# A two-layer decoder trunk on one Trainium2 core: twelve pairs of feed-forward units a layer by seven products, with their weight sums built in scratch memory by accumulating GpSimd transfers

## The chip, the cores and the metric

One core of one Trainium2 chip runs the kernel. The metric is device time in microseconds (us). The kernel before has a median of 1816.6 us in three runs (1816.02, 1816.82, 1816.6). Engines are called as the profile calls them: PE is TensorE (PEld its weight loads), DVE is VectorE, ACT is ScalarE, POOL is GpSimd, and SP is the queue that issues most transfers.

## The reference

Two layers, each on 512 tokens of width 1024 in float32:

```python
h = rmsnorm(x, pre_mix_g)
proj = h @ w_in                                  # q,k,v,z | b,a | q,k,v | gates A, B
y_a = deltanet_branch(...) @ w_up_dn             # 8 heads, gated delta rule in chunks
y_b = swa_sink_branch(...) @ w_up_sw             # 16 heads, window 128
mix = (sigmoid(gate_a) * y_a + sigmoid(gate_b) * y_b) @ w_o
x = x + rmsnorm(mix, post_mix_g)
h2 = rmsnorm(x, pre_mlp_g)
ff = square(relu(h2 @ w_ff1)) @ w_ff2            # 1024 -> 4096 -> 1024
x = x + rmsnorm(ff, post_mlp_g)
```

## The kernel before

All matmuls work on pairs of numbers: a value x is split into a high part (rounded to the format of the fast matmul) and a low part x - high, and a product is the sum of high by high, low by high and high by low. So a plain matrix product is three matmuls per block of 128 rows of the weight (`mm_a`, lines 400 to 402: 512 columns each). Weights come from DRAM in blocks of 128 x 1024 floats (512 KB), one transfer on SP each (`load`, line 282), into one of six buffers `wr`; ACT makes the high part `wh` (line 384) and DVE the low part `wl` (line 385). `weights()` does that four blocks ahead of use (`LOOK`).

A layer runs so: the attention and beta columns of `w_in`; 16 steps of `MIX`, in which the key columns (K), the gate columns (G) and (GA) of `w_in` are multiplied while groups of attention heads run between them (POOL masks the probabilities there, line 1017, tile `pc`); `w_up_sw` (`ps_us`); then the eight delta heads; `w_up_dn` (`ps_ud`); `w_o` with its normalisation; and the feed-forward part.

**The delta heads.** For each head h a chain of four chunks runs through PE, DVE and PE again: `ps_y` (line 1264) to `yy` (DVE, line 1266) to `ps_su` (line 1269) to the state `St` (DVE, line 1272) to `ps_ks` (line 1258) to `rr` (DVE, line 1261) to the next `ps_y`. Between these small matmuls stand matmuls of the next heads' projections (`ps_vp`, `ps_qp`, `ps_zp`) or, in the last head, of the gate (`ps_ga`), so that PE has work while DVE answers. A head's result is normalised by a factor that travels through memory (`d_tail`): `ps_w` sums the squares, `sd<-w` and `ff<-sd` (SP) turn the row into 128 x 4, POOL raises it to a power (line 1215) and stores it (`fd<-ff`, line 1216, the only transfer that POOL issues), `fb<-fd` (SP, line 1219) spreads it over 128 partitions, and DVE multiplies (`yf<-yf,fb`, line 1220). The next head but one does the last step. ACT and DVE then split the result into `yT_h` and `yT_l` (lines 500 and 501) for `w_up_dn`, whose first four units take heads 0 to 5 first (4 x 6 x 3 = 72 matmuls), and then heads 6 and 7.

**The feed-forward part.** `w_ff1` has 32 units of 128 columns, in four slices s = 0 to 3 of eight. Slices 0 to 2 are multiplied by their part of `w_ff2` by seven products instead of eight (`lefts`, `mm_c`). Units of `w_ff1` are multiplied plainly, or two at a time by seven products (`ff1`, `mm_h`): with x0, x1 the two halves of the first unit and x2, x3 those of the second, the seven products need, beside x0, x1 and x3, the sums x0+x2, x0+x2+x3, x0+x1+x2+x3 and x2+x3. `up_specs` loads both units and lets DVE build the sums in two more `wr` buffers (line 343, four additions of 128 x 512 a pair). `SEQ` says which units are pairs: none in slice 0, two in slice 1, three in slice 2 and four in slice 3, nine a layer.

**What sets the order.** The kernel is traced in program order, and a scheduler then places each engine's instructions by its own estimate of when they are ready; a few chains are fixed by hand (`Order`). Transfers on SP wait for the data they need and also for the eighth transfer before them (the waits on DMAHW0 to 7 in the listings below). An engine takes its instructions strictly in order, so one that waits holds all behind it.

## Time and profile before

| what | value |
|---|---|
| runs before (median of 3) | 1816.6 us (1816.02 to 1816.82) |
| the profiled execution | 1816.19 us, its span 1814.5 us |
| PE, PEld busy | 1794.6 us (99%), 1524.7 us (84%) |
| DVE, ACT, POOL busy | 1375.1 us (76%), 1007.5 us (56%), 210.6 us (12%) |
| transfers | 278.60 MB, mean 154 GB/s |
| weight blocks of 512 KB | 320, median 3.6 us from issue to landing |

The span is the time from the first to the last instruction of the profiled execution; its own time holds 1.7 us more. Shares of busy time are averages; what a stretch is bound by is read from that stretch. A row of the timeline gives the start in us, the duration in us (matmuls overlap, so the pace is read from the starts), engine, line, operation, output <- inputs, shape, and in brackets the idle time before it and what ended that.

### The profile page before, as it was taken

What the parts mean: (1) busy time and instruction counts of PE and PEld (TensorE: products, weight loads), DVE (VectorE), ACT (ScalarE), POOL (GpSimd) and SP (SyncE); (2) the same over time, 40 slices, a digit from 0 to 9 for tenths busy, and PEclk for the clock granted to TensorE, in tenths of its full rate; (3) what the DMA queues carried; (4) which work ended last, traced back from release to release, by engine and by line L of the source; (5) the groups of instructions that cost most, each with busy time, mean ns of one, the idle gap of its engine ahead of it and who ended that gap; (6) DMA issues with size and microseconds to landing.
All of it is one profiled execution on the core that took longest, in us unless ns stands there. A gap on an engine that the chain in (4) does not pass through costs nothing.

```text
span 1814.5 us, 28394 instructions
## 1 busy us (share of the span) xinstructions
PE 1794.6 (99%) x10252; PEld 1524.7 (84%) x10252; DVE 1375.1 (76%) x2590; ACT 1007.5 (56%) x2065; POOL 210.6 (12%) x386
## 2 busy tenths in 40 slices
PE   9999999999999999999999999999999999999998
PEld 8878878888788888989898887888877888889896
DVE  5499796887666878898556997968875669698973
ACT  6678742444434656566556877234443347566572
POOL 0322102221101000000013221022111010000000
PEclk9999999999999999999999999999999999999999
DMA  5633447655463254554445334585545533555551
GB/s 201 203 112 121 111 146 226 178 172 152 117 208 129 82 164 156 174 180 145 168 160 176 106 127 111 169 232 159 163 140 154 171 116 105 174 162 164 174 178 56
DMA packets 146431, 278.60 MB, mean 154 GB/s; under 512 B 33569, under 2 KB 66657, under 8 KB 146290
## 3 DMA queue, kind: packets, MB, share of 16 engines
q1 hardware_dynamic: 145778, 276.75, 49.2%
q8 instruction: 81, 1.33, 0.3%
q14 instruction: 60, 0.49, 0.1%
q0 software_dynamic: 512, 0.03, 0.0%
HBM read 239.38 MB, written 37.36 MB: 153 GB/s over the span
## 4 chain that ended last, share of the span: by engine, by line
PE 88%; DVE 4%; ACT 4%; DMA 2%; issue 1%; POOL 0%; SPq 0%; DVEq 0%; POOLq 0%; ACTq 0%
PE ps_b L459 3%; PE ps_b L461 3%; PE ps_b L463 3%; PE ps_f L400 2%; PE ps_f L401 2%; PE ps_f L402 2%; PE ps_us L400 2%; PE ps_ud L400 2%; PE ps_us L401 2%; PE ps_ud L401 2%; PE ps_ud L402 2%; PE ps_us L402 2%; PE ps_vp L400 2%; PE ps_vp L402 2%; PE ps_vp L401 1%; PE ps_qp L401 1%
## 5 line engine op out<-in xcount | busy, mean ns | idle before, releaser
L384 ACT CAST wh<-wr 128x1024 fp32r<-128x1024 f32 (+2 forms) x368 | 372.7, 1019 | 430.4 <-PE ps_us L401 60.2
L385 DVE TENSOR_TENSOR wl<-wr,wh 128x1024 fp32r<-128x1024 f32 (+2 forms) x368 | 434.9, 1189 | 183.8 <-ACT wh L384 180.2
L526 POOL TENSOR_TENSOR pr<-pq,pw 128x1 f32<-128x1 f32 x16 | 9.8, 615 | 790.1 <-DVE pq L525 790.1
L459 PE MATMUL ps_b<-wh,h_h 128*128 128x432 f32 (+1 forms) x192 | 71.1, 370 | 0.0
L461 PE MATMUL ps_b<-wl,h_h 128*128 128x432 f32 (+1 forms) x192 | 70.4, 367 | 0.0
L463 PE MATMUL ps_b<-wh,h_l 128*128 128x432 f32 (+1 forms) x192 | 70.3, 366 | 0.0
L400 PE MATMUL ps_f<-g_h,wh 128*128 128x512 f32 x160 | 62.4, 390 | 0.0
L401 PE MATMUL ps_f<-g_l,wh 128*128 128x512 f32 x160 | 62.4, 390 | 0.0
L402 PE MATMUL ps_f<-g_h,wl 128*128 128x512 f32 x160 | 62.2, 389 | 0.0
L401 PE MATMUL ps_qp<-h_l,wh 128*128 128x512 f32 x128 | 53.9, 421 | 0.0
L400 PE MATMUL ps_vp<-h_h,wh 128*128 128x512 f32 x128 | 53.7, 420 | 0.0
L402 PE MATMUL ps_vp<-h_h,wl 128*128 128x512 f32 x128 | 53.7, 419 | 0.0
L995 ACT ACTIVATE M<-M,nm 128x128 f32<-128x128 f32 x128 | 49.8, 391 | 5.9 <-DVE nm L990 5.8
L400 PE MATMUL ps_qp<-h_h,wh 128*128 128x512 f32 x128 | 51.8, 405 | 0.0
L343 DVE TENSOR_TENSOR wr<-wr 128x512 f32<-128x512 f32 x72 | 47.5, 685 | 5.5 <-DMA wr<-in_weights_dram 5.2
L400 PE MATMUL ps_kp<-h_h,wh 128*128 128x512 f32 x128 | 51.6, 403 | 0.0
L402 PE MATMUL ps_qp<-h_h,wl 128*128 128x512 f32 x128 | 51.4, 401 | 0.0
L401 PE MATMUL ps_vp<-h_l,wh 128*128 128x512 f32 x128 | 51.3, 401 | 0.0
L401 PE MATMUL ps_ga<-h_l,wh 128*128 128x512 f32 x128 | 51.0, 398 | 0.0
L400 PE MATMUL ps_gb<-h_h,wh 128*128 128x512 f32 x128 | 51.0, 398 | 0.0
L402 PE MATMUL ps_kp<-h_h,wl 128*128 128x512 f32 x128 | 50.9, 398 | 0.0
L402 PE MATMUL ps_ga<-h_h,wl 128*128 128x512 f32 x128 | 50.7, 396 | 0.0
(435 smaller groups left out, 5928.4 us busy)
## 6 DMA issues: line engine op xcount, KB each, us to landing
wr<-in_weights_dram SPq DMA_DIRECT2D x320, 512.0 KB, 3.6
wr<-in_weights_dram SPq DMA_DIRECT2D x24, 432.0 KB, 5.2
D<-dd SPq DMA_DIRECT2D x32, 256.0 KB, 2.7
xd<-xo SPq DMA_DIRECT2D x12, 512.0 KB, 3.0
xt<-xd SPq DMA_DIRECT2D x24, 256.0 KB, 4.5
D<-gd SPq DMA_DIRECT2D x16, 256.0 KB, 6.2
dd<-D SPq DMA_DIRECT2D x16, 256.0 KB, 5.2
kkd<-kk SPq DMA_DIRECT2D x16, 256.0 KB, 2.0
```

Source lines behind the costliest of these rows:

```text
L343: tt(out=o_, in0=i0, in1=i1, op=ALU.add)
L384: nc.scalar.copy(wh[:, :w], wr[:, :w])
L385: sub(out=wl[:, :w], in0=wr[:, :w], in1=wh[:, :w].bitcast(F32), op=ALU.subtract)
L400: mm(ps, lhsT=wh[:, k, :], rhs=hi, start=k == 0, stop=False)
L401: mm(ps, lhsT=wh[:, k, :], rhs=lo, start=False, stop=False)
L402: mm(ps, lhsT=wl[:, k, :], rhs=hi, start=False, stop=k == KT - 1)
L459: mm(pss[t], lhsT=hi[:, tsl], rhs=wh[:, r, :], start=k == 0 and not onto, stop=False, skip_group_check=onto)
L461: mm(pss[t], lhsT=hi[:, tsl], rhs=wl[:, r, :], start=False, stop=False, skip_group_check=onto)
L463: mm(pss[t], lhsT=lo[:, tsl], rhs=wh[:, r, :], start=False, stop=k == KT - 1, skip_group_check=onto)
L526: ptt(out=r, in0=q1, in1=mhalf[:, 0:1], op=ALU.pow)
L995: act(out=M[:, j * P:(j + 1) * P], in_=M[:, j * P:(j + 1) * P], func=AF.Exp, bias=nm[:, j:j + 1], accum_out=den[:, j:j + 1])
```

## The change

`SEQ` makes pairs of all units in slices 1 and 2 too: twelve pairs a layer, six more in all. The sums aren't built by DVE any more. For each pair a tile `sums[l, s, pair]` of 128 x 2048 floats lies in DRAM. It is made in four steps (`prepare`): SP copies both units into it (two transfers of 512 KB from DRAM to DRAM); POOL adds to its second and fourth quarter, by one accumulating transfer, the first halves of the units (512 KB); POOL adds one quarter of the tile to another (256 KB); and once more. What stands in it then are the four sums. `unit(ms[0])` and the two halves of the tile are loaded as blocks of 512 KB, and the second half of the second unit as one of 256 KB.

`ready = prepare(l)` does one step for each of up to four pairs at a time, so that one `next(ready)` issues up to two copies on SP and three transfers on POOL. The fifteen calls stand in `MIX` (steps 1, 4, 7, 10), in two places of `w_up_sw`, at the start of heads 1, 3, 5 and 7, in two places of `w_up_dn` and in three of slice 0. `tc.keep_in_program_order` ties each of these transfers behind the instruction of its engine that was traced just before it; those traced after it are not tied. Besides, two halves of a block change places (`n1` and `n2`), the first left factor `P1` is made as soon as its units are there, and two pairs of PSUM banks change their pools in slices 1 and 2.

```diff
--- before.py
+++ after.py
@@ -42,7 +42,8 @@
 WR = 6
 FF_ORDER = (0, 4, 1, 5, 2, 6, 3, 7)
 XB = 6
-SEQ = (FF_ORDER, (0, 1, (4, 5), (2, 3), 6, 7), ((0, 1), (4, 5), (2, 3), 6, 7), ((0, 1), (2, 3), (4, 5), (6, 7)))
+FF_PAIRS = ((0, 1), (4, 5), (2, 3), (6, 7))
+SEQ = (FF_ORDER, FF_PAIRS, FF_PAIRS, ((0, 1), (2, 3), (4, 5), (6, 7)))
 
 MIX = "G K K G K K G K K G K K G GA GA GA".split()
 NA = sum(c.count("A") for c in MIX)
@@ -328,22 +329,19 @@
         def one(ms):
-            b = {}
-
-            def raw():
-                b["0"], b["1"] = (unit(m) for m in ms)
-                return b["0"]
-
-            def of(n_):
-                b[n_] = wp.tile([P, 1024], F32, name="wr", bufs=WR)
-                x0, x1, x2, x3 = b["0"][:, :512], b["0"][:, 512:], b["1"][:, :512], b["1"][:, 512:]
-                yb = b["a"][:, 512:]
-                for o_, i0, i1 in (((b[n_][:, :512], x0, x2), (yb, b[n_][:, :512], x3)) if n_ == "a" else
-                                   ((b[n_][:, 512:], x2, x3), (b[n_][:, :512], yb, x1))):
-                    tt(out=o_, in0=i0, in1=i1, op=ALU.add)
-                return b[n_]
-
-            return raw, lambda: of("a"), lambda: of("b"), lambda: b["1"][:, 512:]
+            d = sums[l, s, ms]
+
+            def of(c, w=1024):
+                wr = wp.tile([P, 1024], F32, name="wr", bufs=WR)
+                dma(wr[:, :w], d[:, c * 1024:c * 1024 + w])
+                return wr
+
+            def tail():
+                wr = wp.tile([P, 1024], F32, name="wr", bufs=WR)
+                dma(wr[:, :512], wpk[index["w_ff1", l, 0, (s * 8 + ms[1]) * P, 0], :, 512:])
+                return wr
+
+            return lambda: unit(ms[0]), lambda: of(0), lambda: of(1), tail
 
         last = None
         for n, e in enumerate(SEQ[s]):
@@ -358,6 +356,35 @@
                 out += [(fa, 0), (fb, 0)]
                 last = tail
         return out + [(last, -1)] * bool(last)
+
+    pairs = [(s_, e) for s_, seq in enumerate(SEQ) for e in seq if isinstance(e, tuple)]
+    sums = {(l, *p): dr.tile([P, 2048], F32, name=f"fs{l}{p[0]}{p[1][0]}")
+            for l in range(depth) for p in pairs}
+
+    def prepare(l):
+
+
+        here = tc.keep_in_program_order
+
+        def stages(s_, e):
+            i = index["w_ff1", l, 0, (s_ * 8 + e[0]) * P, 0]
+            assert index["w_ff1", l, 0, (s_ * 8 + e[1]) * P, 0] == i + 1
+            v = sums[l, s_, e][:, :].rearrange("p (h t c) -> p h t c", h=2, t=2)
+            for t in range(2):
+                here(dma(v[:, :, t, :], wpk[i + t].rearrange("p (h c) -> p h c", h=2)))
+            yield
+            here(pdma(v[:, :, 1, :], wpk[i:i + 2, :, 0:512].rearrange("t p c -> p t c"),
+                      accum_op=ALU.add))
+            yield
+            here(pdma(v[:, 0, 0, :], v[:, 1, 1, :], accum_op=ALU.add))
+            yield
+            here(pdma(v[:, 1, 0, :], v[:, 0, 0, :], accum_op=ALU.add))
+
+        todo = [stages(*p) for p in pairs]
+        for n in range(len(todo) + 3):
+            for g in todo[max(n - 3, 0):n + 1]:
+                next(g, None)
+            yield
 
     specs = []
     for kind_, *key in chunk_order(depth):
@@ -1041,7 +1068,10 @@
 
 
         late, klate = (), []
+        ready = prepare(l)
         for i in range(16):
+            if i in (1, 4, 7, 10):
+                next(ready)
             us = []
             for c in MIX[i]:
                 u = kind[c](n_[c])
@@ -1299,6 +1329,8 @@
             stt(out=mb, in0=sgb[m], scalar=1.0, in1=ps, op0=ALU.add, op1=ALU.mult)
             dma(mbd[m], mb)
             steps(2 if m < 6 else 40)
+            if m in (1, 4):
+                next(ready)
             if m == 1:
                 turn0()
         for m in range(NA, NA2):
@@ -1314,6 +1346,8 @@
             d_decay(h)
             d_turn(h)
         for h in range(H):
+            if h % 2:
+                next(ready)
             if h < H - 2:
                 d_keys(h + 2)
             d_inverse(h)
@@ -1340,6 +1374,8 @@
             first.append((ps, mm_a(ps, yT, range(6))))
         mT = []
         for m in range(KT):
+            if m in (1, 5):
+                next(ready)
             if m % 4 == 0:
                 mq = UQ("mbr")
                 sq = UQ("sgr") if m < NA2 else None
@@ -1504,13 +1540,13 @@
                     return c
 
                 c2 = weights()
-                mm_h(y, c2, 4, ops["n2"], False)
+                mm_h(y, c2, 0, ops["n2"], False)
                 nc.scalar.copy(z, y)
                 mm_h(a, c1, 4, ops["a12"], False)
                 act(out=R[:, half(0)], in_=a, func=AF.Relu)
                 if n > 0:
                     c3 = seventh()
-                mm_h(z, c2, 0, ops["n1"], False)
+                mm_h(z, c2, 4, ops["n1"], False)
                 if n == 0:
                     c3 = seventh()
                 act(out=R[:, half(3)], in_=z, func=AF.Copy, scale=-1.0)
@@ -1542,7 +1578,6 @@
             def lefts(X, Y):
 
                 a11, a21, a12, a22 = X[:, 0:512], X[:, 512:1024], Y[:, 0:512], Y[:, 512:1024]
-                make("P1", T[5], a11)
                 s1, s2 = T[4]("S1"), T[4]("S2")
                 tt(out=s1, in0=a21, in1=a22, op=ALU.subtract)
                 make("P5", T[7], s1)
@@ -1571,6 +1606,8 @@
                     act(out=r_, in_=ps.rearrange("p (a n) -> p a n", a=2), func=AF.Relu)
                     act(out=r_, in_=r_, func=AF.Square)
                 count[0] += len(ms)
+                if ms[-1] in (1, 3):
+                    make("P1", T[5], raw[0][:, 0:512])
                 if count[0] % 4 == 0:
                     lefts(*raw)
 
@@ -1583,12 +1620,13 @@
                         mm_a(ps, h2)
                     done((m,), ps)
                     if s == 0 and i in (1, 3, 5):
+                        next(ready, None)
                         next(cg)
             else:
                 ff1(done, pending)
-            pa = [PZ("ps_pa") for t in range(2)]
+            pa = [(PM if s else PZ)("ps_pa") for t in range(2)]
             mm_c(pa, left["P1"])
-            py = [PM("ps_py") for t in range(2)]
+            py = [(PZ if s else PM)("ps_py") for t in range(2)]
             for t in range(2):
                 act(out=py[t], in_=pa[t], func=AF.Copy, scale=-1.0)
             make_later("P2", T[5])
```

**How the order moves in the delta heads.** PE in head 3, from the first `ps_su` to the second `ps_y`; before:

```order
1725 L1269 MATMUL ps_su<-yy,kd 128x128
1726 L1276 MATMUL ps_o<-aT,yy 128x128
1727 L402 MATMUL ps_vp<-h_h,wl 128x512
1728 L400 MATMUL ps_vp<-h_h,wh 128x512
1729 L401 MATMUL ps_vp<-h_l,wh 128x512
1730 L402 MATMUL ps_vp<-h_h,wl 128x512
1731 L1258 MATMUL ps_ks<-St,kk 128x128
1732 L1259 MATMUL ps_o<-qe,St 128x128
1733 L400 MATMUL ps_vp<-h_h,wh 128x512
1734 L401 MATMUL ps_vp<-h_l,wh 128x512
1735 L1264 MATMUL ps_y<-rr,Pt 128x128
```

and after (lines are 30 higher there, those of `mm_a` 27):

```order
1733 L1299 MATMUL ps_su<-yy,kd 128x128
1734 L1306 MATMUL ps_o<-aT,yy 128x128
1735 L428 MATMUL ps_vp<-h_l,wh 128x512
1736 L429 MATMUL ps_vp<-h_h,wl 128x512
1737 L1288 MATMUL ps_ks<-St,kk 128x128
1738 L1289 MATMUL ps_o<-qe,St 128x128
1739 L427 MATMUL ps_qp<-h_h,wh 128x512
1740 L428 MATMUL ps_qp<-h_l,wh 128x512
1741 L1294 MATMUL ps_y<-rr,Pt 128x128
```

The first `ps_y` of that head is row 1719 before and row 1727 after: eight more matmuls of the projection stand ahead of it. Between `ps_o` and `ps_ks` two matmuls stand where four stood. Counted from head 2's `ps_w` to this `ps_y`, the number of projection matmuls goes from 41 to 42.

DVE in the same head, from the first `yy` to the second; before:

```order
645 L1266 COPY yy<-ps_y 128x128 [waits PE_49]
646 L385 TENSOR_TENSOR wl<-wr,wh 128x1024 [waits Activation_49]
647 L1272 COPY St<-ps_su 128x128 [waits PE_49]
648 L1220 TENSOR_TENSOR yf<-yf,fb 128x512 [waits DMAHW5_49]
649 L1261 SCALAR_TENSOR_TENSOR rr<-ps_ks,neg,vs 128x128 [waits PE_49,Activation_49]
650 L1266 COPY yy<-ps_y 128x128 [waits PE_49]
```

and after:

```order
644 L1296 COPY yy<-ps_y 128x128 [waits PE_49]
645 L1250 TENSOR_TENSOR yf<-yf,fb 128x512 [waits DMAHW2_49]
646 L1302 COPY St<-ps_su 128x128 [waits PE_49]
647 L1291 SCALAR_TENSOR_TENSOR rr<-ps_ks,neg,vs 128x128 [waits PE_49,Activation_49]
648 L412 TENSOR_TENSOR wl<-wr,wh 128x1024 [waits Activation_49]
649 L1296 COPY yy<-ps_y 128x128 [waits PE_49]
```

`yf<-yf,fb`, which waits for a transfer, stood behind `St` and now stands ahead of it; the split `wl` went behind `rr`. It is so in heads 2, 3 and 4 of both layers; in heads 5 and 6 `yf` stays behind `St`, and in head 7 it was ahead of it before as well.

**How the order moves at the end of the heads.** SP from head 7's `sd<-w` to the loads for `w_up_dn`; before:

```order
268 L1211 DMA sd<-w 1x512 [waits Activation_49]
269 L282 DMA wr<-in_weights_dram 128x1024 [waits DMAHW5_49,DVE_49]
270 L1348 DMA mbr<-mbd 128x512 [waits DMAHW6_49,PE_49]
271 L1214 DMA ff<-sd 128x4 [waits DMAHW7_49,DMAHW4_49,Pool_49]
272 L1219 DMA fb<-fd 128x512 [waits DMAHW0_49,DMASW6_49]
273 L1351 DMA sgr<-gad 128x512 [waits DMAHW1_49,PE_49]
274 L1348 DMA mbr<-mbd 128x512
275 L1351 DMA sgr<-gad 128x512 [waits DMAHW3_49]
```

and after (`fs` is a tile of sums; these two copies were traced in `w_up_dn`):

```order
299 L1241 DMA sd<-w 1x512 [waits DMAHW4_49,Activation_49]
300 L1387 DMA sgr<-gad 128x512 [waits DMAHW5_49,PE_49]
301 L1249 DMA fb<-fd 128x512 [waits DMAHW6_49,DMASW6_49]
302 L374 DMA fs_122<-in_weights_dram 256x512 [waits DMAHW7_49]
303 L1244 DMA ff<-sd 128x4 [waits DMAHW4_49,Pool_49]
304 L374 DMA fs_122<-in_weights_dram 256x512 [waits DMAHW1_49]
305 L1384 DMA mbr<-mbd 128x512 [waits DMAHW2_49]
306 L1387 DMA sgr<-gad 128x512 [waits DMAHW3_49]
```

Head 7's `ff<-sd` stood ahead of head 6's `fb<-fd`; now it stands behind that and behind a copy, and another copy follows. In heads 3 and 5 two copies stand near the reload of the keys and values (`kvx<-vxd`) and ahead of `fb<-fd`: in head 3 one on each side of the reload, in head 5 both behind it.

PE there, around head 6's `ps_w`; before:

```order
2186 L1264 MATMUL ps_y<-rr,Pt 128x128
2187 L1208 MATMUL ps_w<-w_h,ones_r 128x512
2188 L1209 MATMUL ps_w<-w_l,ones_r 128x512
2189 L400 MATMUL ps_ga<-h_h,wh 128x512
2190 L1276 MATMUL ps_o<-aT,yy 128x128
2191 L401 MATMUL ps_ga<-h_l,wh 128x512
```

and after:

```order
2193 L1294 MATMUL ps_y<-rr,Pt 128x128
2194 L1238 MATMUL ps_w<-w_h,ones_r 128x512
2195 L1239 MATMUL ps_w<-w_l,ones_r 128x512
2196 L428 MATMUL ps_ga<-h_l,wh 128x512
2197 L1306 MATMUL ps_o<-aT,yy 128x128
2198 L429 MATMUL ps_ga<-h_h,wl 128x512
```

The first `ps_ud` is row 2228 in both, so head 6's `ps_w` is followed by 36 gate matmuls before and by 29 after. Of the 15 that now stand behind the first of head 7's two `ps_w`, ten stand behind the second; it was 22 and 20.

## Prediction

> **What bounds the kernel now.** I read the page's totals and chain first, then stretches of time, then TensorE's waits, and last the timelines of the places that the change touches. The totals:
>
> ```profile
> span 1814.5 us, 28394 instructions
> ...
> PE 1794.6 (99%) x10252; PEld 1524.7 (84%) x10252; DVE 1375.1 (76%) x2590; ACT 1007.5 (56%) x2065; POOL 210.6 (12%) x386
> ...
> q1 hardware_dynamic: 145778, 276.75, 49.2%
> ...
> PE 88%; DVE 4%; ACT 4%; DMA 2%; issue 1%; POOL 0%; SPq 0%; DVEq 0%; POOLq 0%; ACTq 0%
> ```
>
> TensorE is busy for 99% of the span and is 88% of the chain. So time is won by giving it fewer columns, and lost by making it wait. By stretches (columns: engine busy, then granted clock, DMA share, GB/s), first the delta heads and then the feed-forward part of layer 0:
>
> ```profile
> 306.00:490.00 184.00, 183.09 (x1262) 148.90 (x1258) 148.26 (x302) 83.17 (x160) 32.27 (x54) 1.00 0.53 148
> ...
> 657.00:843.00 186.00, 186.00 (x1094) 165.79 (x1093) 158.76 (x198) 113.15 (x171) 0.00 (x0) 1.00 0.48 154
> ```
>
> In the feed-forward part TensorE never stops: 186.00 of 186.00. In the heads it does, a little. Three rows of its waits name who can stop it near the change:
>
> ```profile
> PE ps_y L1264 <- DVE rr L1261: 1.2, 2, 0.7
> PE ps_y L1264 <- ACT vs L1247: 0.9, 1, 0.9
> ...
> PE ps_o L1023 <- POOL pc L1017: 0.6, 1, 0.6
> ```
>
> **The change, part by part. Six more pairs.** Nine pairs a layer become twelve: two more in slice 1 and one more in slice 2, six over both layers. Plain matmuls of 512 columns and those of 256 in a pair follow each other like this on PE:
>
> ```profile
> 659.62 0.39 PE L477 MATMUL ps_pw<-wl,P_h 128*128 128x512 f32 x1
> ...
> 664.15 0.39 PE L400 MATMUL ps_f<-g_h,wh 128*128 128x512 f32 x1
> ...
> 741.73 0.28 PE L487 MATMUL ps_a<-g_h,wh 128*128 128x256 f32 x1
> ...
> 742.33 0.28 PE L490 MATMUL ps_a<-g_h,wl 128*128 128x256 f32 x1
> ```
>
> Twenty steps from 659.62 to 664.15 are 0.2267 us each, five from 741.73 to 742.33 are 0.120 us. Two plain units are 2 x 8 row blocks x 3 products = 48 matmuls, 10.88 us. A pair is 7 products x 4 x 3 = 84, 10.08 us. That is 0.80 us a pair, **-4.8 us** for six, all on the path.
>
> **The sums leave VectorE.**
>
> ```profile
> L343 DVE TENSOR_TENSOR wr<-wr 128x512 f32<-128x512 f32 x72 | 47.5, 685 | 5.5 <-DMA wr<-in_weights_dram 5.2
> ```
>
> All 72 go, 47.5 us, but in stretches where TensorE never waits: nothing. In their place a pair loads 1.83 MB (three tiles of 0.52 and one of 0.26) where it loaded 1.05; twelve pairs in some 180 us add 9.4 MB, 52 GB/s to the 154 above. I take nothing for that, nor for the earlier P1, the swapped halves and the swapped PSUM pools: the 186.00 of 186.00 says that no wait is there to be moved. If that cover goes, a late tile costs its wait once per pair.
>
> **POOL in the groups of attention.** The accumulating transfers stand among the selects that TensorE waits for. The tightest place has three of them after the second of these rows; the third row is the one transfer that POOL issues in before:
>
> ```profile
> 168.56 0.64 POOL L1017 TENSOR_SCALAR_AFFINE_SELECT pc<-pf_l 128x512 fp32r<-128x512 f32 x1 [0.16 <-DVE pf_l L501]
> 172.25 0.64 POOL L1017 TENSOR_SCALAR_AFFINE_SELECT pc<-pf_h 128x512 fp32r<-128x512 f32 x1 [3.05 <-ACT pf_h L500]
> ...
> 486.09 0.62 POOL L1216 DMA_DIRECT2D fd<-ff  x1 [0.29 <-POOL ff L1215]
> ```
>
> Three issues by 0.62 us are 1.9 in a gap of 3.05: nothing. This transfer is 2 KB and the new ones 256 to 512 KB, so the upper end is the price at which the gap overflows, below among the rivals.
>
> **The order in the delta heads.** This is where I expect the change to be paid. The front part shows it: in heads 2, 3 and 4 the factor `yf<-yf,fb` moves ahead of `St` on DVE (in head 7 it stood there already), and TensorE runs two matmuls instead of four between the `ps_o` after `ps_su` and `ps_ks`. Head 3 of layer 0 before, on PE, DVE and SP:
>
> ```profile
> 377.13 0.38 PE L1264 MATMUL ps_y<-vs,Pt 128*128 128x128 f32 x2
> ...
> 379.87 0.39 PE L1258 MATMUL ps_ks<-St,kk 128*128 128x128 f32 x2
> ```
>
> ```profile
> 377.86 0.28 DVE L1266 COPY yy<-ps_y 128x128 f32<-128x128 f32 x1
> ...
> 379.19 0.28 DVE L1272 COPY St<-ps_su 128x128 f32<-128x128 f32 x1
> 379.39 0.68 DVE L1220 TENSOR_TENSOR yf<-yf,fb 128x512 f32<-128x512 f32 x1
> ```
>
> ```profile
> 370.74 0.32 SPq L1153 DMA_DIRECT2D kvx<-vxd  x1
> ...
> 374.47 0.47 SPq L1219 DMA_DIRECT2D fb<-fd  x1
> ```
>
> `ps_ks` follows `ps_y` by 2.74 us; with two matmuls fewer it is due at 2.74 - 0.45 = 2.29. The broadcast `fb` is issued 2.66 before `ps_y`, one matmul more in after, so 2.89. How long does it take to land?
>
> ```profile
>   DMA fb<-fd: 23.4, 10
> ...
> DMA to landing us min/median/max: 4.7/4.8/4.9
> ```
>
> The second row says 4.8, from few recorded landings; the first, DVE's idle time before the factors, that they are waited for already. Counting from `ps_y`, `fb` is there at 4.8 - 2.9 = 1.9, `yf` ends at 2.6 and `St` at 2.87: TensorE waits 0.6 us and a hand-over, 0.65. The ends come from two other heads, in which DVE waited for `fb`:
>
> ```profile
> 444.56 0.32 SPq L1219 DMA_DIRECT2D fb<-fd  x1
> ...
> 1295.27 0.44 SPq L1219 DMA_DIRECT2D fb<-fd  x1
> ```
>
> ```profile
> 448.28 0.69 DVE L1220 TENSOR_TENSOR yf<-yf,fb 128x512 f32<-128x512 f32 x1 [0.49 <-DMA fb<-fd]
> ...
> 1301.31 0.69 DVE L1220 TENSOR_TENSOR yf<-yf,fb 128x512 f32<-128x512 f32 x1 [1.02 <-DMA fb<-fd]
> ```
>
> At 3.7 us (444.56 to 448.28) `fb` is early and nothing waits; at 6.0 (1295.27 to 1301.31) the wait is 1.8, of which that head already paid 0.7 at `ps_y`, the longest in the first row of waits. So five heads by 0.65 and one by 1.1: **+4.4 us**, between 0 and 6 x 1.8 - 0.7 = 10. In head 7 eight more matmuls (1.8 us) come before the first `ps_y`, which waited 0.9 for `vs`: **-0.9 us**, or 0 if copies delay its load.
>
> **Copies on SP.** In heads 3 and 5 two copies of 512 KB come between the reload of `kvx` and `fb`. 276.75 MB took 49.2% of 16 engines' 1814.5 us, 51.6 engine-us a MB, so a copy of 0.52 MB is 1.7 us on all sixteen, counted once. Before, SP issues the reload at 370.74 and `fb` at 374.47; two copies (3.4 us of traffic) put in behind the reload have 2.9 us before `fb`, which leaves 0.5. That is for head 5 in both layers, **+1.0 us**; in head 3 one of the two goes ahead of the reload and I take nothing. Ends: 0, and a whole copy in all four, 6.8.
>
> [...]
>
> **The tail of head 7.** Its normalisation has to be back before `w_up_dn` needs head 7:
>
> ```profile
> 480.31 0.48 PE L1208 MATMUL ps_w<-w_h,ones_r 128*128 128x512 f32 x1
> ...
> 489.85 0.39 PE L400 MATMUL ps_ud<-yT_h,wh 128*128 128x512 f32 x1
> ...
> 1389.17 0.39 PE L400 MATMUL ps_ud<-yT_h,wh 128*128 128x512 f32 x1
> ```
>
> ```profile
> 488.07 0.35 SPq L1214 DMA_DIRECT2D ff<-sd  x1
> 489.36 0.32 SPq L1219 DMA_DIRECT2D fb<-fd  x1
> ```
>
> ```profile
> 503.64 1.29 DVE L501 TENSOR_TENSOR yT_l<-yf,yT_h 128x512 fp32r<-128x512 f32 x2 [0.20 <-DVE yf L1220]
> ...
> 1403.47 1.29 DVE L501 TENSOR_TENSOR yT_l<-yf,yT_h 128x512 fp32r<-128x512 f32 x2 [0.20 <-DVE yf L1220]
> ```
>
> The low part is ready at 504.93; its first user is the 77th matmul, 489.85 + 76 x 0.227 = 507.1: 2.2 us of slack, and 1.7 in layer 1 (1404.76 against 1406.4). After, head 6's `ps_w` stands 7 matmuls nearer to the end (29 instead of 36), so its `fb` leaves SP at 489.36 + 1.6 = 490.96. Head 7's `ff<-sd` now stands behind that `fb` and a copy: two issues of 0.4, so 491.8 instead of 488.07, 3.7 late. TensorE waits 1.5 and 2.0: **+3.5 us**. It is 0 if what follows is quicker by 2, and 2 x 1.7 more if the copies are in the way of `ff` and `fb`.
>
> **Sum.** -4.8 + 4.4 - 0.9 + 1.0 + 3.5 = +3.2 us. On the profiled execution's 1816.19 that is 1819.4; the median of the runs, 1816.6, lies 0.4 above it: **1819.8 us**. What a measurement of this kernel can tell from no change is about 0.2%, 3.6 us, so the bounds are 1813.0 and 1820.2.
>
> **The rivals.** *The gain with few waits.* The broadcasts land like the one of 3.7 us and head 7's chain catches up: -4.8 - 0.9 and 0 to 1 of waits, **1811 us**. For it: TensorE waits little in the heads before, and most new distances are no shorter. Against: the recorded landings of 4.7 to 4.9, and the 23.4 us that DVE already idles before those factors.
>
> *Copies in the way, slower.* Each copy costs the small transfer behind it a full 1.7 us: four broadcasts (+6.8 instead of 1.0) and head 7's `ff` or `fb` in each layer (+3.4): 1819.8 + 9.2 = **1829 us**. It decides from about 0.25 us per copy on (3.2 - 1.0 + 6 x 0.25 = 3.7 is past the bound). For it speaks the 6.0 row; against it the 2.9 us of head start and DMA engines that are half idle.
>
> *POOL late.* If issuing a transfer holds POOL 1.2 us longer, three take 5.5 in the gap of 3.05, and TensorE waits 2.4 for the select, once a layer: 1819.8 + 4.8 = **1824.6 us**. [...]
>
> *No gain.* The pairs don't save their 0.8 us, because a tile of sums comes late in slice 1: 1819.8 + 4.8, also 1824.6, or about the time before where the heads cost nothing. The pairs of slice 3 speak against it.
>
> **How the numbers follow.** The forecast has 0.40, its own range being 1814 to 1824: of it 0.22 within 0.2%, 0.15 slower, 0.03 faster. Few waits: 0.32, 0.30 of it faster and 0.02 same. Copies: 0.18, slower. POOL: 0.06, 0.04 slower and 0.02 same. No gain: 0.04, half same, half slower. Together faster 0.33, same 0.28, slower 0.39. Below 1810.5 lies about a third of the second case, above 1829 half of the third: the range is 1810.5 to 1829.
>
> **What would show it.** Right: the stretch of the feed-forward part is 2.4 us shorter in each layer with TensorE still full; in heads 2, 3 and 4 `ps_ks` waits for `St`, and DVE before it for `fb`; the first `ps_ud` that uses head 7 waits for `yT_l`. Wrong: no such waits (then the time is near 1811), or waits for `pc` in the groups, or for `wr` in slice 1.

## The result and the profile after

The changed kernel takes 1876.1 us (median of four runs, 1871.8 to 1878.3) against 1816.7 for the kernel before beside it (1816.0 to 1818.3): 1.0323 times as long, 95% interval 1.0300 to 1.0345. That is slower by 59 us. The prediction named this sign as its likeliest single one (0.39), but with 1819.8 us and a range that ended at 1829. The profiled execution of after is the fastest of its four, 1871.77 us.

The totals of the page of after, and three of its DMA issues (the last columns: KB each, us to landing):

```profile
span 1870.0 us, 29142 instructions
...
PE 1805.4 (97%) x10468; PEld 1541.3 (82%) x10468; DVE 1348.1 (72%) x2542; ACT 1024.3 (55%) x2101; POOL 291.0 (16%) x458
...
PE 74%; DMA 8%; DVE 8%; ACT 4%; issue 3%; POOL 2%; SPq 0%; DVEq 0%; POOLq 0%; ACTq 0%
...
fs<-in_weights_dram SPq DMA_DIRECT2D x48, 512.0 KB, 6.3
...
fs<-in_weights_dram POOLq DMA_DIRECT2D x24, 512.0 KB, 10.7
fs<-fs POOLq DMA_DIRECT2D x48, 256.0 KB, 7.1
```

PE is busy for 97% of the span instead of 99%, and it fell from 88% to 74% of the chain; DMA went from 2% to 8%, DVE from 4% to 8%, POOL from 0% to 2%. An accumulating transfer takes 7 to 11 us from issue to landing. By stretches of layer 0: heads, `w_up_dn`, feed-forward part; first before, then after (columns as in the prediction: us, engines busy, granted clock, DMA share, GB/s):

```profile
301.26:489.85 188.59, 187.68 (x1366) 152.58 (x1361) 152.56 (x312) 84.36 (x163) 32.56 (x55) 1.00 0.54 151
489.85:555.29 65.44, 65.44 (x289) 53.99 (x288) 34.03 (x44) 21.53 (x30) 1.62 (x2) 1.00 0.60 196
578.85:862.85 284.00, 283.79 (x1701) 254.21 (x1700) 241.20 (x301) 180.06 (x281) 3.46 (x4) 1.00 0.47 154
```

```profile
302.38:512.70 210.32, 193.98 (x1367) 157.66 (x1362) 152.41 (x312) 84.68 (x163) 49.80 (x67) 0.97 0.68 188
512.70:586.15 73.45, 67.57 (x289) 55.01 (x288) 34.12 (x44) 21.60 (x30) 7.22 (x8) 0.98 0.72 209
609.71:892.39 282.68, 282.18 (x1809) 257.38 (x1808) 227.54 (x277) 188.46 (x299) 8.70 (x10) 1.00 0.63 195
```

The heads are 21.7 us longer and `w_up_dn` 8.0; the feed-forward part is 1.3 shorter. In layer 1 it is the same: heads 190.4 to 211.6, `w_up_dn` 65.4 to 71.3, feed-forward part -1.1. So all of the loss but 1.5 us (`MIX` of layer 0, 169.33 to 170.80) lies in the delta heads and in `w_up_dn` behind them. It has two kinds. PE is idle longer: in the heads of layer 0 by 210.32 - 193.98 = 16.3 us where it was 0.9. And it is busy longer for as many matmuls (1367 against 1366): 193.98 against 187.68, at a granted clock of 0.97. Over both layers, heads and `w_up_dn`, 42 us are idle time and 15 are slower matmuls.

What PE waits for in after, and DVE for the factor:

```profile
PE ps_ks L1288 <- DVE St L1302: 23.1, 8, 4.2
PE ps_ud L428 <- DVE yT_l L528: 11.2, 4, 4.6
PE ps_y L1294 <- DVE rr L1291: 9.3, 3, 5.7
...
PE ps_o L1050 <- POOL pc L1044: 1.1, 2, 0.6
```

```profile
DVE yf L1250 <- DMA fb<-fd: 72.4, 16, 14.2
```

The first two rows are the waits that the prediction named: `St` behind `yf` on DVE, which waits for `fb`, and `yT_l` in `w_up_dn`. Their size is another: 4.2 us at most instead of 0.65, and DVE idles 72.4 us before the factors instead of 23.4.

Why is `fb` late? Head 2's factor travels from `ps_w` to `yf`. Here is its way before, on SP and POOL:

```profile
392.54 0.37 SPq L1214 DMA_DIRECT2D ff<-sd  x1
```

```profile
394.40 1.04 POOL L1215 TENSOR_TENSOR ff<-ff,pw 128x4 f32<-128x4 f32 x1 [4.15 <-DMA ff<-sd]
395.73 0.62 POOL L1216 DMA_DIRECT2D fd<-ff  x1 [0.29 <-POOL ff L1215]
397.00 0.68 POOL L1137 COPY T<-Tc 32x128 f32<-32x128 f32 x2 [0.65 <-PE ps_i L1098]
```

and after, on SP, POOL, DVE and PE:

```profile
402.14 0.37 SPq L1244 DMA_DIRECT2D ff<-sd  x1
...
410.99 0.34 SPq L1249 DMA_DIRECT2D fb<-fd  x1
```

```profile
405.73 1.59 POOL L1167 COPY T<-Tc 32x128 f32<-32x128 f32 x2 [4.15 <-PE ps_i L1128]
407.40 1.37 POOL L1245 TENSOR_TENSOR ff<-ff,pw 128x4 f32<-128x4 f32 x1
409.19 0.65 POOL L1246 DMA_DIRECT2D fd<-ff  x1 [0.42 <-POOL ff L1245]
```

```profile
416.68 0.69 DVE L1250 TENSOR_TENSOR yf<-yf,fb 128x512 f32<-128x512 f32 x1 [4.59 <-DMA fb<-fd]
417.29 0.28 DVE L1302 COPY St<-ps_su 128x128 f32<-128x128 f32 x1
```

```profile
417.63 0.80 PE L1288 MATMUL ps_ks<-St,kk 128*128 128x128 f32 x2 [4.16 <-DVE St L1302]
```

Before, POOL raises `ff` to its power 1.86 us after SP issued the load (392.54 to 394.40), and copies `T<-Tc` afterwards. After, the copies stand first. They wait for `ps_i`, a result of the inverse in the next head but one, and the power begins 5.26 us after the load was issued (402.14 to 407.40). POOL takes its instructions in order (the power begins 0.08 us after the copies end), so 3.4 us are lost there; the prediction's lists show PE, DVE and SP, and not POOL. Everything behind it is late by as much, down to PE: SP issues `fb` at 410.99, and `ps_y` of the head that needs it starts at 411.00, so the broadcast has no head start at all.

At the end of layer 0's heads, on POOL, SP, DVE and PE of after (the last row's bracket is PE's wait):

```profile
522.26 0.63 POOL L1246 DMA_DIRECT2D fd<-ff  x1 [0.30 <-POOL ff L1245]
522.89 0.94 POOL L381 DMA_DIRECT2D fs<-fs  x1
523.47 1.22 POOL L379 DMA_DIRECT2D fs<-fs  x1
524.02 1.74 POOL L376 DMA_DIRECT2D fs<-in_weights_dram  x1
```

```profile
525.68 0.32 SPq L1249 DMA_DIRECT2D fb<-fd  x1
```

```profile
534.07 0.69 DVE L1250 TENSOR_TENSOR yf<-yf,fb 128x512 f32<-128x512 f32 x1 [14.24 <-DMA fb<-fd]
```

```profile
535.71 0.80 PE L428 MATMUL ps_ud<-yT_l,wh 128*128 128x512 f32 x1 [4.63 <-DVE yT_l L528]
```

Three accumulating transfers of 1 MB together start right ahead of the broadcast `fb`, which then takes 8.39 us until `yf` can begin (525.68 to 534.07). Before it took 4.90 there; in layer 1 it is 8.14 against 4.72.

So there are two suspects, POOL's order and the traffic. The theory put to the test first was the order; its rival, that the new transfers stand beside the small ones.

### The profile page after: what moved, and what is told of

Same layout as the page of the kernel before. It is cut to its first block, busy times and chain, and to the rows that moved or that the text cites. A ratio compares the mean times of both kernels' runs of the same rounds, so it can differ in the third digit from the quotient of the medians.

```text
span 1870.0 us, 29142 instructions
## 1 busy us (share of the span) xinstructions
PE 1805.4 (97%) x10468; PEld 1541.3 (82%) x10468; DVE 1348.1 (72%) x2542; ACT 1024.3 (55%) x2101; POOL 291.0 (16%) x458
## 4 chain that ended last, share of the span: by engine, by line
PE 74%; DMA 8%; DVE 8%; ACT 4%; issue 3%; POOL 2%; SPq 0%; DVEq 0%; POOLq 0%; ACTq 0%
DMA fb<-fd 3%; PE ps_b L486 3%; PE ps_b L488 3%; PE ps_b L490 3%; DMA fd<-ff 2%; PE ps_us L427 2%; PE ps_us L428 2%; PE ps_us L429 2%; PE ps_qp L427 2%; PE ps_qp L428 2%; PE ps_qp L429 1%; DVE wl L412 1%; PE ps_z L514 1%; PE ps_o L1050 1%; PE ps_a L517 1%
## 5 line engine op out<-in xcount | busy, mean ns | idle before, releaser
L486 PE MATMUL ps_b<-wh,h_h 128*128 128x432 f32 (+1 forms) x192 | 71.1, 370 | 0.0
L1250 DVE TENSOR_TENSOR yf<-yf,fb 128x512 f32<-128x512 f32 x16 | 11.1, 692 | 72.4 <-DMA fb<-fd 72.4
L428 PE MATMUL ps_ud<-yT_l,wh 128*128 128x512 f32 x128 | 51.1, 399 | 11.2 <-DVE yT_l L528 11.2
L829 ACT ACTIVATE th<-vv 128x512 f32<-128x512 f32 x16 | 10.1, 632 | 87.8 <-DVE vv L826 87.8
L514 PE MATMUL ps_z<-n_h,wh 128*128 128x256 f32 x192 | 54.9, 286 | 0.0
L517 PE MATMUL ps_a<-g_h,wl 128*128 128x256 f32 x192 | 54.3, 283 | 0.0
L516 PE MATMUL ps_a<-g_l,wh 128*128 128x256 f32 x192 | 54.3, 283 | 0.0
L517 PE MATMUL ps_z<-n_h,wl 128*128 128x256 f32 x192 | 54.3, 283 | 0.0
L516 PE MATMUL ps_z<-n_l,wh 128*128 128x256 f32 x192 | 54.3, 283 | 0.0
L514 PE MATMUL ps_a<-g_h,wh 128*128 128x256 f32 x192 | 54.3, 283 | 0.0
L427 PE MATMUL ps_ga<-h_h,wh 128*128 128x512 f32 x128 | 51.8, 405 | 0.5 <-ACT sga L884 0.5
```

The costliest lines, as they stand in the source:

```text
L427: mm(ps, lhsT=wh[:, k, :], rhs=hi, start=k == 0, stop=False)
L428: mm(ps, lhsT=wh[:, k, :], rhs=lo, start=False, stop=False)
L486: mm(pss[t], lhsT=hi[:, tsl], rhs=wh[:, r, :], start=k == 0 and not onto, stop=False, skip_group_check=onto)
L514: mm(ps, lhsT=wh[:, k0 + k, :], rhs=hi, start=start and k == 0, stop=False, skip_group_check=True)
L516: mm(ps, lhsT=wh[:, k0 + k, :], rhs=lo, start=False, stop=False, skip_group_check=True)
L517: mm(ps, lhsT=wl[:, k0 + k, :], rhs=hi, start=False, stop=k == 3, skip_group_check=True)
```

## The experiments

The lengths below are read from the first matmul of a stage to that of the next, in one profiled execution each, in us (layer 0 / layer 1):

| kernel | time, median | heads | `w_up_dn` | feed-forward |
|---|---|---|---|---|
| before | 1816.7 | 188.6 / 190.4 | 65.4 / 65.4 | 284.0 / 284.0 |
| pairs_only | 1814.5 | 188.1 / 188.9 | 66.9 / 66.9 | 283.8 / 282.7 |
| quiet | 1814.2 | 189.1 / 188.8 | 65.4 / 65.9 | 282.7 / 282.7 |
| order_dve | 1833.0 | 196.2 / 198.2 | 67.2 / 66.7 | 283.4 / 282.8 |
| order_pool | 1838.0 | 203.1 / 203.5 | 65.4 / 65.6 | 282.7 / 282.7 |
| order_only | 1843.9 | 202.0 / 204.5 | 66.7 / 67.1 | 283.0 / 282.7 |
| copies_only | 1852.1 | 204.9 / 205.1 | 68.8 / 69.5 | 282.7 / 282.7 |
| adds_heads | 1823.3 | 195.8 / 189.9 | 67.2 / 68.7 | 282.9 / 282.7 |
| tied | 1868.9 | 203.4 / 201.2 | 71.1 / 75.6 | 282.7 / 282.7 |
| after | 1876.1 | 210.3 / 211.6 | 73.5 / 71.3 | 282.7 / 282.9 |

The lengths are those of the one profiled execution, which needn't be a median one: it took 1856.1 us of tied and 1842.0 of order_pool.

**pairs_only: the pairs without the preparing transfers.** `prepare` yields and does nothing, and a pair loads plain blocks in place of its sums:

```diff
-                dma(wr[:, :w], d[:, c * 1024:c * 1024 + w])
+                dma(wr[:, :w], wpk[index["w_ff1", l, 0, (s * 8 + ms[c % 2]) * P, 0], :, :w])
...
-        todo = [stages(*p) for p in pairs]
+        todo = []
```

> Twelve pairs a layer, but no transfer prepares a sum: the tiles of sums are loaded from the plain weights instead, so the pairs multiply other numbers in the same number of instructions. On every engine the delta heads stand as in the kernel before. Theory (the order in the heads, that the transfers brought about, is what costs) and rival (the transfers cost by sharing the DMA engines) both expect the gain of the pairs and nothing else: 1816.7 - 4.8, and up to 2 us of small waits in the feed-forward part: 1812 to 1814 us.

1814.5 us, 0.9987 of before (0.9978 to 0.9996), half a microsecond above what was expected. The heads have the order of before, on POOL too. So the pairs are worth 2.3 us (0.7 to 4.0 by the interval), and the order of the heads comes from the transfers.

**order_only: POOL's order of after, without the transfers.** pairs_only, with ties that only set an order: `T<-Tc` ahead of the power, and `yf` ahead of `St` in heads 2, 3 and 4. POOL's order then is that of after. PE's and SP's move most of the way, not all of it: in the first heads some projection matmuls, and on SP some small transfers (`fb` among them), still stand elsewhere than in after.

```diff
+                    if ("pow", h - 2) in dn and h >= 3:
+                        tie(dn["pow", h - 2], x_)
...
+            if h + 2 in (2, 3, 4):
+                tie(dn["st0", h + 2], last_)
```

> As pairs_only (no preparing transfers, plain weights in the place of sums), but with the changed kernel's order in the heads, forced by ties: POOL's two copies into T ahead of the power of ff, and DVE's yf ahead of St in heads 2, 3 and 4. Theory (order): the power comes 3.8 us later in three heads a layer and TensorE waits some 4 us there, plus the tail: 1812 + 24 + 4 = 1840 us. Rival (contention): without transfers this order costs no more than 0.65 us a head, so 1812 to 1818 us.

1843.9 us, 1.0145 of before (1.0129 to 1.0160). Without a byte of new traffic in the heads, this order costs 29.4 us over pairs_only. The rival's 1812 to 1818 is out as the only cause. But after is 32 us slower still, so this order isn't the only cause either.

**tied: after with the order put right.** All transfers stay, and PE's order too; the first `T<-Tc` stands behind the power and `yf` behind the first `St`.

```diff
+                    if ("pow", h - 2) in dn:
+                        tie(x_, dn["pow", h - 2])
...
+            if h + 2 < H:
+                tie(last_, dn["st0", h + 2])
```

> The changed kernel with two ties in the heads: the first copy into T stands behind the power of ff on POOL, and yf behind the first St on DVE. All transfers stay where they are, TensorE's order too. Theory (order): the 3.8 us in six heads go, and about 0.5 us each from yf: 1876 - 25 = 1850 us. Rival (contention): the transfers are still beside ff and fb, 1868 to 1876 us.

1868.9 us, 1.0304 of before (1.0287 to 1.0321): 7 us better than after by medians, which isn't clear of the noise (the executions of tied lie between 1856 and 1875 us, those of after between 1872 and 1878), where the order had cost 29. The theory's number missed, and the rival came closer. The order isn't wholly put right, though: one of the two copies `T<-Tc` now stands between the power and its store `fd`. The two causes don't add. What holds up the factor of head 1 in layer 0 of this kernel, on SP and on POOL:

```profile
373.34 0.50 SPq L374 DMA_DIRECT2D fs<-in_weights_dram  x1
...
380.39 0.32 SPq L1256 DMA_DIRECT2D fb<-fd  x1
```

```profile
373.78 1.03 POOL L1252 TENSOR_TENSOR ff<-ff,pw 128x4 f32<-128x4 f32 x1 [2.93 <-DMA ff<-sd]
...
375.22 0.64 POOL L1253 DMA_DIRECT2D fd<-ff  x1
```

The power is early now, but the 2 KB of `fd`, sent at 375.22 behind a copy, lead to `fb` only 5.17 us later (2.0 to 2.3 in heads 1 to 3 before), and `fb` itself takes 6.7.

**quiet: the whole change, with the steps elsewhere.** The fifteen steps of `prepare` stand in seven places of `MIX` and eight of slices 0 to 2; none in `w_up_sw`, the heads or `w_up_dn`.

```diff
-            if i in (1, 4, 7, 10):
+            if i in (1, 3, 5, 7, 9, 11, 13):
                 next(ready)
...
-            if h % 2:
-                next(ready)
...
+                if count[0] in (2, 4, 6):
+                    next(ready, None)
```

> The changed kernel in full, but the fifteen steps of preparing stand in other places: seven in the attention groups (every second one), three each in slices 0 and 1 and two in slice 2, none in w_up_sw, the heads and w_up_dn. In the heads all engines stand as in the kernel before. Theory (order, and what hits the heads): near pairs_only, 1812 to 1816 us. Rival (the 70 MB more cost wherever they are): a third or more of the 59 us stays, 1836 us or more.

1814.2 us, 0.9984 of before (0.9975 to 0.9994): as expected, far below after and 2.6 us below before. The order of the heads is that of before. This row of PE's waits is the only one in the heads or in `w_up_dn` of over half a microsecond:

```profile
PE ps_y L1294 <- ACT vs L1277: 2.0, 2, 1.1
```

So the same transfers cost nothing that can be measured when they stand in `MIX` and in the slices, and the gain of the pairs is kept.

**order_pool and order_dve: which engine's order.** pairs_only with one of the two ties of order_only each:

```diff
 order_pool
+                        tie(dn["pow", h - 2], x_)
 order_dve
+                tie(dn["st0", h + 2], last_)
```

> As order_only, but only POOL's part of the order is forced: the two copies into T, which wait for ps_i from TensorE, stand ahead of the power of ff in three heads a layer; TensorE and DVE keep the order of before. If POOL's order makes the cost: the power comes 3 us late in six heads, yf is still behind St, so rr waits 2 to 3 us: 1814.5 + 15 = 1830 us. If DVE's order makes it: at most 1818 us.

> As order_only, but only DVE's part is forced: yf ahead of St in heads 2, 3 and 4; TensorE's order then moves as in the changed kernel by the scheduler's own choice, and POOL's copies into T stand ahead of the power in one more head than before. If POOL's order makes the cost: 6 waits of 0.65 us for yf and one late power a layer, 1814.5 + 4 + 6 = 1825 us. If DVE's order makes it: 1840 us or more, all of order_only.

order_pool: 1838.0 us, 1.0110 of before (1.0092 to 1.0127), against 1830 expected of POOL and 1818 or less if DVE's order were the cause. PE keeps the order of before there, DVE too but for one instruction a layer, and SP but for four small transfers a layer. So POOL's order, with the little that moved with it, costs 23.5 us over pairs_only. order_dve: 1833.0 us, 1.0095 (1.0077 to 1.0112), between its two expectations; it isn't clean, because POOL's copies go ahead of the power in four tails of it too. In the heads it differs from order_only in one thing alone: the power of head 1 is early. The two kernels lie 10.9 us apart, so that is what this place in POOL's order costs, with nothing else changed there. Head 3, which has `yf` ahead of `St` and still an early power, takes 23.58 and 23.20 us in its two layers (from its first `ps_qk` to that of head 4) against 23.29 before. So `yf` ahead of `St`, with PE's order, costs 0 to 0.3 us as long as `fb` isn't late.

**copies_only: after without the accumulating transfers.**

```diff
-            here(pdma(v[:, :, 1, :], wpk[i:i + 2, :, 0:512].rearrange("t p c -> p t c"),
-                      accum_op=ALU.add))
...
-            here(pdma(v[:, 0, 0, :], v[:, 1, 1, :], accum_op=ALU.add))
```

> The changed kernel without the accumulating transfers of POOL: SP's copies stay, so the tiles hold plain weights and not sums. The order in the heads is that of the changed kernel. Order alone gave 1844, the changed kernel 1876: the 32 us between are the transfers. If SP's copies make them (they stand in SP's queue ahead of ff, fb and kvx): 1866 us or more. If POOL's accumulating transfers make them: 1850 us.

1852.1 us, 1.0189 of before (1.0172 to 1.0207). The order of the heads is that of after on every engine: it is the copies on SP, pinned between `w_up_sw` and `w_up_dn`, that make the scheduler place POOL's work so, and not the transfers on POOL. On top of order_only, the copies cost 8 us, and what of the order order_only lacks is in these 8. Putting the accumulating transfers back costs 24 more. In the tail of head 7 `fb` takes 4.4 and 4.5 us without them, no more than before, and 8.4 and 8.1 with them. Summed over the sixteen factors, the step from the issue of `ff` to POOL's power is as long with them as without (62.6 and 61.8 us), but that from the issue of `fb` to `yf` is 84.1 and 70.2. So they lengthen the way of the broadcast, and not POOL's step.

**tail_free: the steps of `w_up_dn` later.** They move from units 1 and 5 to 4 and 6.

```diff
-            if m in (1, 5):
+            if m in (4, 6):
                 next(ready)
```

> The changed kernel with the two steps of w_up_dn moved from its units 1 and 5 to its units 4 and 6, so that the copies aren't issued among the last heads' small transfers. If these copies make the wait at the first ps_ud of head 7 (14 us in both layers, 3 of it by the order alone): 1876 - 9 = 1867 us. If what was issued before them makes it: 1873 us or more.

1877.8 us, 1.0331 of before (1.0311 to 1.0351). No better than after, and the time that the copies' theory asked for didn't come. The copies did move: SP issues the first at 521.7 us in place of 514.5. But the second goes out at 529.4, right behind `fb`, so this run alone doesn't clear the copies; copies_only, where `fb` is quick, does. The accumulating transfers didn't move:

```profile
524.19 0.63 POOL L1246 DMA_DIRECT2D fd<-ff  x1 [0.30 <-POOL ff L1245]
524.83 0.94 POOL L381 DMA_DIRECT2D fs<-fs  x1
```

They are tied behind POOL's instruction before them in the program, and that is head 7's `fd<-ff` at whichever unit they are traced. So they start ahead of `fb` here as well, and `fb` takes 7.5 and 10.6 us in the two layers.

**adds_heads: the accumulating transfers in the heads, the copies in `MIX`.** One pair's copies in each of steps 1 to 12 of `MIX`; POOL's transfers in two places of `w_up_sw`, heads 1, 3, 5 and 7, two of `w_up_dn` and on into the slices.

```diff
-            if i in (1, 4, 7, 10):
-                next(ready)
+            if 0 < i < 13:
+                next(copies)
```

> The full computation: the copies of all pairs stand in the attention groups (one pair a step), the accumulating transfers stay in w_up_sw, the heads, w_up_dn and slices 0 and 1. In the heads all engines keep the order of before, POOL's with the accumulating transfers between. The changed kernel with copies alone gave 1852, with both 1876, so the accumulating transfers cost 24 there. If they cost that by sharing the DMA engines, whatever the order: 1814 + 15 to 24 = 1829 to 1838 us, with fb of head 7 landing 3 us later or more. If they cost it only where the order had left no slack: 1814 to 1820 us.

1823.3 us, 1.0036 of before (1.0020 to 1.0052), between the two expectations. The order of the heads is that of before. So the accumulating transfers cost about 9 us over quiet with that order, and 24 with the order of after. One broadcast in layer 0 and the two of head 7 met them:

```profile
374.64 2.29 SPq L1254 DMA_DIRECT2D fb<-fd  x1
```

```profile
375.90 0.89 POOL L386 DMA_DIRECT2D fs<-fs  x1
376.47 1.17 POOL L384 DMA_DIRECT2D fs<-fs  x1
377.01 1.70 POOL L381 DMA_DIRECT2D fs<-in_weights_dram  x1
```

```profile
384.58 0.49 PE L1299 MATMUL ps_y<-rr,Pt 128*128 128x128 f32 x2 [3.44 <-DVE rr L1296]
```

SP issued `fb` at 374.64, POOL its three transfers at 375.90 to 377.01; `yf` could begin 8.94 us after `fb` was issued, and PE waited 3.44.

**unpinned: after without the pins.**

```diff
-        here = tc.keep_in_program_order
+        here = lambda x: x
```

> The changed kernel without the pins: the scheduler is free, and puts nearly all copies and accumulating transfers of both layers ahead of the first attention groups, the heads keep the order of before. Theory: nothing is lost in the heads, but POOL, which takes its instructions in order, waits there for the landing of each transfer before the next (7 to 11 us each) and holds the selects of the first groups: 1814 + 30 or more, in layer 0's groups. Rival: the transfers are over before the first selects matter, 1814 to 1818 us.

1998.5 us, 1.0990 of before (1.0966 to 1.1014). The scheduler moves all transfers of both layers into the front of layer 0 (17 to 361 us), most of POOL's ahead of its first mask:

```profile
PE ps_o L1050 <- POOL pc L1044: 109.0, 11, 67.7
```

POOL's masks stand behind a row of transfers, and PE waits 109 us for them, of the 184 us that this kernel takes more than quiet. The heads take 188.3 and 189.1 us there, as before. So transfers on POOL do stop TensorE for what POOL owes it, where enough of them stand in a row; after, with the pins, has 1.1 us of that wait.

## Why the prediction was wrong, point by point

**The step that failed** is "The order in the delta heads", +4.4 us, and with it the tail, +3.5. Both took the way of a factor (`ps_w`, `sd`, `ff`, power, `fd`, `fb`, `yf`) as long as before, and asked only where on DVE and SP its last part would stand. So the sum let `fb` leave 2.89 us ahead of the first `ps_y`. In heads 3 and 4 of after, which use the factors of heads 1 and 2, it leaves 0.01 to 0.17 us ahead, and `ps_ks` waits 3.5 to 4.2 us in place of 0.65. The way from `ps_w` to `yf` had 14.3 us before in a usual head. For the factors of heads 1 to 3 it has 17.3 to 19.9 in after: from the issue of `ff` on, the power comes 3.4 to 3.9 us later than before. order_pool, with PE's order unchanged, is 23.5 us over pairs_only. Where the power stays early, in head 3 of order_dve, `ps_ks` waits 0.2 us and nothing: there the prediction's price for `yf` ahead of `St` was even too high. That the change came out slower, as the likeliest sign said, is no proof of the sum: the time is lost to another cause. The order of POOL's instructions, `T<-Tc` ahead of the power, was to be read from the same listing as the three engines that the prediction did look at.

**The transfers in the heads.** "Copies on SP" had +1.0 and the accumulating transfers nothing. Measured on top of the order of after, copies cost 8 us and accumulating transfers 24. The rival "Copies in the way" asked the right question, with 1.7 us for each copy and 1829 us in all, but left out the accumulating transfers. In the tail of head 7 in layer 0 `fb` on SP took 8.4 us instead of 4.9 with POOL's transfers issued right ahead of it, and 4.4 with them taken out. The broadcast of 3.7 us (444.56 to 448.28), on which the rival "The gain with few waits" rested, wasn't alone: SP issued `egb` 0.36 us behind it (444.92), and the DMA engines were busy for 0.61 of its time, against 0.75 for the one of 6.0.

**The clock.** The prediction counted waits, and not what comes after them. The 15 us by which PE is busy longer in heads and `w_up_dn` come with its long waits, eight of 3.25 to 5.70 us: the trace of after has a granted clock of 0.50 in eight stretches there, 30.7 us together, and half of that is 15.4. The trace of before has no such stretch from 13 to 1809 us, and its mean clock is 0.999, as in pairs_only and quiet. That of order_pool is 0.992 over 1840.3 us, 14.7 us lost against 1.8 in pairs_only, so that by this estimate about half of what its order costs is the slower clock. The last section has the rows.

**The tail** was placed rightly: the first `ps_ud` of head 7 waits for `yT_l`. But it had another size and another cause. `w_up_dn` is longer by 8.0 and 5.9 us, not by 1.5 and 2.0. The issues that moved on SP, from which the prediction had its number, aren't shown to cost anything: order_only is longer by 1.3 and 1.7, but pairs_only, with the order of before, by 1.5 in both (the `fb` of head 6 takes 6.6 and 6.5 us there, 4.7 before). With the copies it is 3.3 and 4.1, and the rest came with the accumulating transfers.

**Head 7's wait for `vs`** is gone from the waits of after, as said.

**The pairs** gave 2.3 us in place of 4.8: the feed-forward part is shorter by 1.3 and 1.1 us, not 2.4 each. The price of a pair was right; the matmuls keep their 0.227 and 0.120 us. What was put at nothing is the change of slices: in quiet 4 matmuls take 1.33 us there (729.76 to 731.09) and not 0.91, where PE waits for `wh`. That comes twice a layer, with 0.1 us at a `ps_z` each time: 2.1 us in all.

**POOL in the groups of attention**: +0 was right for layer 1 (169.36 to 169.42 us for `MIX`), 1.5 short for layer 0 (169.33 to 170.80). "POOL late" was rightly given little. Its 1.2 us more for each issue, three of them 5.5 us together, stand in no run: in after the three kinds of accumulating issue hold POOL for 0.87, 1.05 and 1.54 us on average, 3.5 together, against 0.65 for `fd`, and PE waits for `pc` 1.1 us in both layers together.

**The sum as measured**, by medians: pairs -2.3, order +29.4, copies +8.2, accumulating transfers +24.0, together +59.3. It is a sum in this sequence only; adds_heads, and less clearly tied, show that in another the parts have other sizes. All three lengthen the same way of the factor, which had little slack to begin with.

**What stays open.** How the copies in the heads would do with the order of before wasn't tried: with them there, the scheduler makes the other one. That the accumulating transfers slow `fb` is shown; that they do it by sharing the DMA engines fits the rows, but no run shows it by itself. Why head 6's `fb` is slow in pairs_only, without new traffic beside it, isn't known.

## What to carry to other kernels

When a chain crosses engines through small transfers, list its order on every engine that it passes, also on the one that is 12% busy: here two small copies ahead of POOL's step, in six heads, cost ten times what the pairs gained. Bulk traffic that nobody waits for belongs where the critical chains are loose: the same transfers cost 62 us in one place (1876.1 against 1814.5 without them) and nothing in another. And a transfer tied to its place moves what isn't tied: the scheduler arranged the rest around it, on an engine that the transfer never touches.

## What the runs showed of the hardware

After a long wait TensorE ran at less than its pace. Before the wait of 4.63 us in the tail of layer 0 matmuls of 512 columns started every 0.227 us; behind it, eight took 3.5 us (535.71 to 539.21), and then the pace was back:

```profile
535.71 0.80 PE L428 MATMUL ps_ud<-yT_l,wh 128*128 128x512 f32 x1 [4.63 <-DVE yT_l L528]
536.30 0.63 PE L429 MATMUL ps_ud<-yT_h,wl 128*128 128x512 f32 x1
536.73 0.63 PE L427 MATMUL ps_ud<-yT_h,wh 128*128 128x512 f32 x1
...
538.87 0.50 PE L429 MATMUL ps_ud<-yT_h,wl 128*128 128x512 f32 x1
539.21 0.39 PE L427 MATMUL ps_ud<-yT_h,wh 128*128 128x512 f32 x1
```

So that wait cost 4.6 us and 1.7 more. It isn't so behind each wait; in layer 1 one of 3.50 us was followed by the full pace:

```profile
1462.39 0.50 PE L428 MATMUL ps_ud<-yT_l,wh 128*128 128x512 f32 x1 [3.50 <-DVE yT_l L528]
1462.73 0.40 PE L429 MATMUL ps_ud<-yT_h,wl 128*128 128x512 f32 x1
1462.96 0.39 PE L427 MATMUL ps_ud<-yT_h,wh 128*128 128x512 f32 x1
```

In the first case that is 0.44 us a matmul, 1.9 times 0.227, for 3.5 us; in the second the matmuls started 0.23 us apart from the second one on. The granted clock (the last column but two) behind the two waits:

```profile
535.70:539.30 3.60, 3.59 (x9) 2.87 (x10) 1.57 (x3) 1.04 (x1) 0.71 (x1) 0.53 1.08 341
1462.40:1466.00 3.60, 3.60 (x16) 3.00 (x17) 2.66 (x4) 2.07 (x3) 1.15 (x2) 1.00 1.08 301
```

The eight stretches at 0.50 in the heads and `w_up_dn` of after last 3.41 us each, but for one of 6.83. Each begins near the end of a wait of PE, from 1.4 us ahead of it to 1.3 us behind it. The length of the wait alone doesn't tell the two cases apart: one of 3.25 us had such a stretch behind it (1423.14 to 1426.55), and the one of 3.50 us had none. What decides isn't shown here.
